# A shift of a matrix by half its rows and columns: both column halves of a row in one DMA

## The chip, the core and the metric

The kernel runs on one core of one Trainium2 chip. It uses no compute engine for its work: the matrix is moved from device memory to device memory by the core's 16 DMA engines, which are told what to copy by instructions ("issues") on a queue of SyncE, called SP in the profile. The metric is the device time of one execution in microseconds. Each kernel is run several times and the median is given. One further execution is taken with the hardware profiler; its trace has a record of every instruction, of every packet that a DMA engine moved, and of every report that a DMA has landed.

## The reference

```python
"x": np.random.randn(8192, 8192).astype(np.float32)

def reference(x: np.ndarray) -> np.ndarray:
    return np.fft.ifftshift(x)
```

With even sizes, the shift moves every element by half the rows and half the columns, round the edge: `out[r, c] = x[(r + 4096) % 8192, (c + 4096) % 8192]`. The four quadrants of the matrix change places across the diagonals. Nothing is calculated. The input has 8192 x 8192 x 4 bytes = 268.4 MB, all of which is read once and written once. A row is 32 KB long; half a row, 16 KB, is contiguous both in the source and in the destination.

## The kernel before

`R` and `C` are the rows and columns, 8192 each; `hr` and `hc` are their halves, 4096 (lines 21 to 23). The loop on line 35 takes `rows = ENGINES * apart` = 64 output rows at a time, 128 times. For each block of 64 rows the loop on line 36 issues four DMAs, one per quarter of the row. A quarter is `piece = hc // 2` = 2048 columns, 8 KB. The quarters are taken in the order of their first output column: 0, `hc`, `piece`, `hc + piece`; that is, the first quarter, the third, the second, the fourth.

Numbering the quarters 0 to 3, the first DMA of a block writes quarter 0 and reads quarter 2 of the rows 4096 further on; the second writes quarter 2 and reads quarter 0; the third writes 1 and reads 3; the fourth writes 3 and reads 1.

The helper `copy` (lines 25 to 29) builds one DMA. Its access pattern has two dimensions, `[[C, rows], [1, piece]]`: 64 rows, 32 KB from one to the next, and 2048 contiguous elements in each. So a DMA holds 64 pieces of 8 KB, 512 KB in all. The 64 rows are divided over the 16 engines, four rows each (`apart = 4`). An engine copies a piece as one packet; after its share of a DMA it writes a small packet that raises the DMA's semaphore by one.

There are 128 x 4 = 512 DMAs, all issued on SyncE's queue, `nc.sync`, in program order; line 26 is the line that the profile gives for an issue. There is no explicit wait in the kernel's text. The tile framework gives the DMAs eight semaphores in turn, and an issue that takes a semaphore again first waits until the DMA that used it eight issues earlier has landed. That is the wait put down to line 26. At the end of the program, line 63, SyncE waits for the last DMAs.

Nothing in the program depends on the order in which DMAs land, as no two of them touch the same bytes.

Of the kernel before, what the change touches and what calls it, by code (L numbers as in the profile page):

```python
# [1 line left out]

# [4 lines left out]


ENGINES = 16  # L10


@with_exitstack
def kernel(
    ctx: ExitStack,
    tc: tile.TileContext,
    x: bass.AP,
    out: bass.AP,
):
    nc = tc.nc  # L20
    R, C = x.shape
    hr = R // 2
    hc = C // 2

    def copy(queue, row, col, dims):
        queue.dma_start(
            out=bass.AP(out.tensor, out.offset + row * C + col, dims),
            in_=bass.AP(x.tensor, x.offset + (row + hr) % R * C + (col + hc) % C, dims),
        )


    apart = 4
    piece = hc // 2
    rows = ENGINES * apart
    for row in range(0, R, rows):
        for col in (0, hc, piece, hc + piece):
            copy(nc.sync, row, col, [[C, rows], [1, piece]])


# [1 line left out]
_INS = ['x']  # L41
_OUTS = [((8192, 8192), 'float32')]


def kernel(**inputs):
    import numpy as _np
    import concourse.bacc as _bacc
    import concourse.tile as _tile
    from concourse import mybir as _mybir
    from concourse.bass_utils import run_bass_kernel_spmd as _run  # L50

    nc = _bacc.Bacc("TRN2", target_bir_lowering=False, num_devices=1)  # L52
    arrays, args = {}, []
    for name in _INS:
        a = _np.ascontiguousarray(inputs[name])
        if a.dtype.kind in "iu":
            a = a.astype(_np.int64)
        arrays[f"in_{name}_dram"] = a
        args.append(nc.dram_tensor(f"in_{name}_dram", a.shape, _mybir.dt.from_np(a.dtype), kind="ExternalInput").ap())
    for i, (shape, dtype) in enumerate(_OUTS):  # L60
        dt = _mybir.dt.from_np(_np.dtype(dtype))
        args.append(nc.dram_tensor(f"out_{i}_dram", shape, dt, kind="ExternalOutput").ap())
    with _tile.TileContext(nc) as tc:
        kernel(tc, *args)
    r = _run(nc, [arrays], core_ids=[0])
    got = tuple(r.results[0][f"out_{i}_dram"] for i in range(len(_OUTS)))
    return got[0]
```

## Time and profile before

| What | Value |
|---|---|
| Median of 3 runs | 813.25 us (812.37 to 813.68) |
| The profiled execution: its own time | 811.93 us |
| The profiled execution: span of the core | 810.2 us |
| Share of the span in which the 16 DMA engines had a packet of the kernel's queue | 99.1% |
| Packets of the kernel's queue | 40,960 |
| Bytes moved per second, one way | 331 GB/s |
| Issues | 512, of 512 KB |
| From issue to landing, median (lowest, highest) | 12.6 us (4.0, 13.2) |
| Time that SyncE's queue waited at line 26 for earlier DMAs | 525.9 us |

How to read it: the span runs from the first instruction of the core to the last; the execution's own time is a little longer, since it has what lies around them. The DMA line of the page cuts the span into 40 equal slices and gives the mean busy share of the 16 DMA engines in each, as a digit in tenths; the line under it gives the bytes that they moved. A packet counts as busy from its start to its end, also while it makes no progress. "GB/s" of the engines counts a copied byte once; the line on the memory counts it twice, as a byte read and a byte written. The waits are those of SyncE's queue; "us in total, times, longest us" follow the colon. The issue line gives the count, the size of one and the median time to its landing. The four GpSimd instructions on the page set constants at the start, and the kernel does not use them.

### The profile page before, as it was taken

Reading aid. Unit: us, or ns where it says so; the run is one execution under the profiler, and the core shown is the slowest. Engines: PE = TensorE matmul, PEld = TensorE weight load, DVE = VectorE, ACT = ScalarE, POOL = GpSimd, SP = SyncE. Lnnn points to the kernel's source line nnn. Section 1 sums busy time; section 2 is a strip of 40 time slices with the busy share of each in tenths; the row PEclk is TensorE's granted clock in tenths of the full one; section 3 lists DMA queues with packets and bytes.
Section 4 is the critical chain, followed back from the end, with each engine's and each line's share of the span. In section 5 each row is a group of like instructions: output and inputs, shape, how many; then the busy total and the mean of one; then the engine's idle time right before and its main releaser. Section 6 shows DMA issues by size and latency. Waiting matters only on the chain. (4 is left out here: it accounts for less than half of the span.)

```text
span 810.2 us, 557 instructions
## 1 busy us (share of the span) xinstructions
POOL 0.2 (0%) x4
## 2 busy tenths in 40 slices
POOL 0000000000000000000000000000000000000000
DMA  8999999999999999999999999999999999999998
GB/s 301 334 328 339 330 335 336 334 329 335 337 336 331 331 335 335 329 335 331 339 333 329 339 336 331 339 330 331 337 336 326 337 330 335 333 328 335 326 328 299
DMA packets 40964, 268.50 MB, mean 331 GB/s; under 512 B 8192, under 2 KB 8192, under 8 KB 8192
## 3 DMA queue, kind: packets, MB, share of 16 engines
q1 hardware_dynamic: 40960, 268.47, 99.1%
q14 instruction: 4, 0.03, 0.0%
HBM read 268.44 MB, written 268.44 MB: 663 GB/s over the span
## 5 line engine op out<-in xcount | busy, mean ns | idle before, releaser
L52 POOL MEMSET const-bfloat16-1.0<- 128x1 bf16 x1 | 0.1, 102 | 0.0
L52 POOL MEMSET const-uint8-127<- 128x1 uint8 x1 | 0.1, 102 | 0.0
L52 POOL MEMSET const-float32-0.0<- 128x1 f32 x1 | 0.1, 99 | 0.2 <-issue 0.2
L52 POOL MEMSET const-float32-1.0<- 128x1 f32 x1 | 0.1, 99 | 0.0
## 6 DMA issues: line engine op xcount, KB each, us to landing
out_dram<-in_x_dram SPq DMA_DIRECT2D x512, 512.0 KB, 12.6
```

Source lines behind the costliest of these rows:

```text
L52: nc = _bacc.Bacc("TRN2", target_bir_lowering=False, num_devices=1)
```

## The change

One DMA now takes the same quarter of both halves of 64 rows. The helper `both` replaces `copy`. Its access pattern has three dimensions: 64 rows; two pieces `hc` columns (16 KB) apart; 2048 contiguous elements. In the destination the second piece lies `hc` columns after the first, in the source `hc` columns before it, since the halves change places. The loop over the columns has two steps, 0 and `piece`, where it had four. So there are 128 x 2 = 256 DMAs of 128 pieces, 1 MB each, on the same queue. The 64 rows are still divided over 16 engines, four rows each, and an engine has eight pieces in a DMA: for each of its rows the piece in the left half of the output and then the piece in the right half.

```diff
-    def copy(queue, row, col, dims):
+    def both(queue, row, col, rows, piece):
+
         queue.dma_start(
-            out=bass.AP(out.tensor, out.offset + row * C + col, dims),
-            in_=bass.AP(x.tensor, x.offset + (row + hr) % R * C + (col + hc) % C, dims),
+            out=bass.AP(out.tensor, out.offset + row * C + col, [[C, rows], [hc, 2], [1, piece]]),
+            in_=bass.AP(
+                x.tensor,
+                x.offset + (row + hr) % R * C + hc + col,
+                [[C, rows], [-hc, 2], [1, piece]],
+            ),
         )
...
     for row in range(0, R, rows):
-        for col in (0, hc, piece, hc + piece):
-            copy(nc.sync, row, col, [[C, rows], [1, piece]])
+        for col in (0, piece):
+            both(nc.sync, row, col, rows, piece)
```

## The prediction

> **What bounds the kernel now.** I read the page from the top: span, share by slice, DMA queue, DMA issues; then SyncE's waits, the windows at the two ends of the span, and last the single packet records.
>
> ```profile
> span 810.2 us, 557 instructions
> ...
> DMA  8999999999999999999999999999999999999998
> ...
> DMA packets 40964, 268.50 MB, mean 331 GB/s; under 512 B 8192, under 2 KB 8192, under 8 KB 8192
> ...
> q1 hardware_dynamic: 40960, 268.47, 99.1%
> ...
> HBM read 268.44 MB, written 268.44 MB: 663 GB/s over the span
> ...
> out_dram<-in_x_dram SPq DMA_DIRECT2D x512, 512.0 KB, 12.6
> ```
>
> No compute engine takes part. The 16 DMA engines have a packet in hand 99.1% of the span, in every slice. 40,960 packets over 512 DMAs are 80 each: 64 pieces of 8 KB and 16 small ones that report completion, one from each engine. A DMA lands 12.6 us after its issue, but 810.2 / 512 = 1.58 us pass per DMA, so 12.6 / 1.58 = 8 are in flight.
>
> ```profile
> SPq L26 <- DMA out_dram<-in_x_dram: 525.9, 502, 2.0
> SPq L63 <- DMA out_dram<-in_x_dram: 11.5, 4, 7.1
> ```
>
> SyncE's queue waits 525.9 us at line 26 for an older DMA to land before it issues the next: it runs ahead and is held back, it does not hold the engines up. The instruction itself takes 511 ns (median for line 26), 512 x 0.511 = 262 us.
>
> ```profile
> 0.73:2.14 1.41, 0.00 (x0) 1.00 0.00 0
> 2.14:3.00 0.86, 0.00 (x0) 1.00 1.19 171
> ...
> 806.00:807.00 1.00, 0.00 (x0) 1.00 0.95 344
> 807.00:808.00 1.00, 0.00 (x0) 1.00 0.74 254
> 808.00:809.00 1.00, 0.00 (x0) 1.00 0.18 74
> 809.00:810.20 1.20, 0.00 (x0) 1.00 0.00 0
> ```
>
> The windows (stretch, length, GpSimd, clock, DMA share, GB/s) show what is not copying: 1.41 us from the first issue to the first packet, a drain of about 2 us as engines run dry one by one, 1.2 us at the end.
>
> "Busy" is not "fast". In the packet records the commonest 8 KB packet takes 309 ns, and 60% take that; 40% take longer, 511 ns on average; the mean is 389.9. Packets of one engine follow each other 3 ns before the end of the last, so with none slow the copy would take 32,768 / 16 x 0.306 = 627 us. The other some 180 us is time in which an engine holds a packet that is held up: (389.9 - 309) x 2,048 = 166 us of it directly. What holds it is outside the engines; that it is the memory is my reading. So the bound is the rate at which memory serves 16 engines that read and write together, 663 GB/s, and the change can matter mainly through the 81 ns of mean excess. The Trainium skill (HBM Reference, Specifications) gives about 716 GB/s for the memory that a core pair shares; 663 is 93% of it, by which an estimate of the least time is 537 MB / 716 = 750 us.
>
> **The change part by part.** Sums are against the profiled execution, 811.93 us (span 810.2 and 1.73 around it), 1.32 us under the median of the three runs, 813.25.
>
> *Issues.* 512 DMAs of 64 pieces become 256 of 128. If the 511 ns go with the pieces, 8 ns each, an issue takes 1.02 us; the engines need 2 x 1.58 = 3.15 us for a DMA, so SyncE still waits some 2.1 us each time. Cost nothing; cover is the copying, and it is gone only if an issue took over 3.15 us. Nothing else is queued on SyncE but the next issue, and the final wait of line 63, which grows from 11.5 us to about 23 with eight DMAs of twice the size in flight, behind copying that must be done anyway.
>
> *Start.* The first packet comes 1.41 us after the first issue began, whose instruction took 0.63. If packets wait until the whole DMA is described, 64 more pieces add up to 0.6; if not, nothing. I take 0.3.
>
> *Completion packets.* 8,192 become 4,096, so 256 fewer on each engine. Each lasts 9 ns, and the next packet starts 6 after its start: 256 x 6 = 1.5 us. Where the memory is the limit, engine time set free turns into waiting, so between 0 and 1.5 (2.3 at 9 ns); by the 60% of packets that go at full pace, I take -0.9. There may be a little more behind them: the 8 KB packets that can be told to follow a completion packet directly take 395 ns, 5 over the mean, 256 x 5.5 = 1.4 us at most. The Trainium skill (DMA: Bandwidth & Descriptors, Rules for kernel authors) speaks for 1 MB or more per DMA, since each has a fixed cost. Were its two microseconds paid 512 times in a row, they would exceed the whole time: here seven other DMAs cover them, and the rows leave only those few microseconds.
>
> *Order of the pieces.* This is what the time hangs on. An engine takes four rows of each DMA. Before, it copies four pieces 32 KB apart in address, then the other half of the same rows, then the next quarter. After, it copies a row's piece and then that row's piece 16 KB further, while the source goes 16 KB back. The bytes, sizes and rows touched by 16 engines in a few microseconds stay nearly alike: the 16 landings of a DMA are 1.76 us apart in the median, longer than a DMA lasts, so engines already mix two DMAs. The alternation within one engine is shown nowhere in the trace, so I bound it by the four kinds of step from one DMA to the next. Sort the 32,768 data packets by start and take the 33rd of each 64 as the middle of a DMA; from middle to middle is (mean of about 123, standard error about 11 ns):
>
> - same rows, other half (columns 0 to hc): 1,564 ns
> - next quarter (hc to piece): 1,573
> - same rows, other half (piece to hc + piece): 1,602
> - next 64 rows: 1,559
>
> Mean 1,574.6. The two steps to the other half of the same rows average 1,583.1, the two others 1,566.1. The difference, 17 ns, is about one and a half standard errors of it: a hint and no proof. The nearest row to the new order is the first pair, where some engines are in one half of the rows and some in the other: if all copying went so, 512 x (1,583.1 - 1,574.6) = +4.4 us. Ends: all like the slowest step, 512 x (1,602 - 1,574.6) = +14; all like the fastest (1,550 for next 64 rows, with the cut three quarters into a DMA), 512 x (1,550 - 1,574.6) = -12.6. I take +4.4, for being the nearest.
>
> *Tail.* Every engine has the same bytes as before. The drain is set by how far engines drift apart, and 1.76 us is far less than the 12.6 us of queue, so the queue does not limit the drift and a longer one does not widen it: 0, at worst another 1.8.
>
> Sum: 0.3 - 0.9 + 4.4 = +3.8; 811.93 + 3.8 = 815.7, and with the 1.32 to the median **817.0 us**.
>
> **The rivals.**
>
> *The order of the pieces is indifferent.* For it: the four steps lie within 2.8% of each other, though columns and rows change differently in each. Then 813.25 + 0.3 - 0.9 = 812.7, within 0.2%, which is 1.6 us and about what a measurement of this kernel can tell from no change. Against it: two percent of 807 us is 16 us, and memory that is held up in 40% of the packets is unlikely not to notice a new order at all.
>
> *The alternation eases the memory (faster).* Two pieces of one row within some 0.8 us instead of 1.6 could be served better than pieces of different rows. Place: the 40% slow packets. Price: if all copying goes like the fastest step, -12.6, with the other terms 813.25 - 12.6 - 0.6 = 800; half of that, 806. It decides from the point where the mean packet falls under about 389 ns, since 1.6 us / 2,048 packets is 0.8 ns. Against it: the steps that stay in the same rows are, if anything, the slower ones, and the step to new rows is the fastest.
>
> *Engines get in each other's way.* With a DMA of eight packets an engine, drift of 4.5 packets (1.76 us / 0.39) keeps all engines within one DMA and one pair of quarters for longer. If the slow packets go from 40% to 44%, the excess grows by a tenth: 8 ns x 2,048 = 17 us, 829; to 50%, 20 x 2,048 = 41 us, 854. For it: the slowest step, 1,602, is one within a pair of quarters. Against it: the other such step takes 1,564.
>
> *The change doesn't do what it says.* Were the pieces split over the two halves and not the rows, two engines would carry a DMA and the time would be several times as long; were an engine given all of one half first, the order would be the old one and the time 812.7.
>
> **How the numbers follow.** Somewhat slower, by up to 14 us and around 817: 0.38. Engines in each other's way, 829 and more: 0.10. Indifferent or the old order, 812.7: 0.18. Faster, 800 to 811: 0.33. A split over few engines: 0.01. So slower 0.49, same 0.18, faster 0.33. The range goes from 801 (the fastest step throughout, 800, nearly) to 830 (the slowest step, +14, start and tail, +2.4, and the lesser price of engines in each other's way); about 0.06 lies below and 0.10 above. The likeliest case alone runs from 815 to 828, the slowest step throughout without tail.
>
> **What would show it.** Packets 32,768 + 4,096 + the four that fetch instructions; 256 issues of 1 MB, landing after about 25 us; an issue of about 1.0 us; SyncE's wait still most of its time. If I am right the mean 8 KB packet takes 392 ns (4.4 us / 2,048 = 2.1 ns more), GB/s drops evenly over the slices to about 330, the DMA share stays at 99%, and the two ends keep their lengths. A first packet after 1.41 + 0.6 us would show the start at its upper end; a drain of 4 us the tail. A mean packet under 389 ns makes the forecast wrong on the fast side; idle engines (a share under 98%) would mean that issues or the queue matter, which I have ruled out.

## The result and the profile after

The changed kernel takes 811.08 us (median of 14 runs, 809.99 to 812.37), the kernel before 813.16 us (14 runs beside them, 811.43 to 816.31). The ratio is 0.9972 with a 95% interval of 0.9964 to 0.9981: the change makes the kernel 0.28% faster, 2.1 us, and the interval stays clear of no change. I had forecast 817.0, that is 0.45% slower.

The page of the changed kernel, the same lines as shown of before:

```profile
span 808.7 us, 301 instructions
...
DMA  8999999999999999999999999999999999999998
...
DMA packets 36866, 268.47 MB, mean 332 GB/s; under 512 B 4096, under 2 KB 4096, under 8 KB 4096
...
q1 hardware_dynamic: 36864, 268.45, 99.3%
...
HBM read 268.44 MB, written 268.44 MB: 664 GB/s over the span
...
out_dram<-in_x_dram SPq DMA_DIRECT2D x256, 1024.0 KB, 25.1
```

The change does what it says: 32,768 data packets as before, 4,096 completion packets in place of 8,192, 256 DMAs of 1 MB that land after 25.1 us, so still eight in flight. The engines have a packet in hand in all slices, and the rate went from 663 to 664 GB/s of reading and writing together. Nothing large moved anywhere.

SyncE's waits after, and the group of its issues before and after (lowest, median and highest duration in ns, first and last start in us):

```profile
SPq L27 <- DMA out_dram<-in_x_dram: 634.0, 248, 3.2
SPq L68 <- DMA out_dram<-in_x_dram: 24.1, 4, 15.2
```

```profile
L26 SPq DMA_DIRECT2D out_dram<-in_x_dram x512: 511/511/695, 0.7 to 797.2; - x171
```

```profile
L27 SPq DMA_DIRECT2D out_dram<-in_x_dram x256: 562/562/682, 0.7 to 783.1; - x128
```

The queue is held back by landings for 634 us, more than before, and the last wait doubled as foreseen. An issue of twice the pieces takes 562 ns, and before it took 511. The number of pieces is not what adds the 51 ns: the old order in 256 DMAs (below) has 128 pieces in a DMA too, in the old pattern of two dimensions, and its issues take 511.

The windows at the two ends (stretch, length, GpSimd, clock, DMA share, GB/s):

```profile
0.73:2.14 1.41, 0.00 (x0) 1.00 0.00 0
2.14:3.00 0.86, 0.00 (x0) 1.00 0.95 162
...
805.00:806.00 1.00, 0.00 (x0) 1.00 0.88 336
806.00:807.00 1.00, 0.00 (x0) 1.00 0.30 123
807.00:808.00 1.00, 0.00 (x0) 1.00 0.02 8
```

The start is as long as before; the drain is some 1.5 us earlier, and about as long. So the gain was made on the way and not at the ends. The single packet records say where, as far as one execution of each can:

| Per engine, profiled execution | Before | After |
|---|---|---|
| First packet's start to last packet's end | 806.90 us | 805.36 us |
| Sum of packet times | 803.06 us | 803.07 us |
| of it completion packets (9 ns each) | 4.6 us | 2.3 us |
| Mean 8 KB packet | 389.9 ns | 391.0 ns |
| 8 KB packets over 312 ns | 40.0% | 40.9% |
| Time with no packet in hand | 11.5 us | 9.2 us |

The last row is an estimate: the first row, less the second, plus 3 ns for each packet of an engine (2,560 and 2,304), by which a packet usually starts before the end of the one before it. By the windows, more than 1 us of it is the drain at the end, before and after. In this execution the 2.3 us of completion packets that are gone came back as longer data packets, 1.13 ns x 2,048 = 2.3 us, and what made it shorter is 2.3 us less of idle moments, less 0.8 us of overlap that went with the fewer packets.

This split is not firm. The three later profiles of the changed kernel have 8.0 us without a packet (chip 2, mean packet 392.0 ns), 8.9 and 7.6 us (chip 9, 396.3 and 397.2 ns). Another kernel of the experiments, the new order in 512 DMAs with two neighbouring rows an engine, has 11.3 us in one profile (chip 9) and 9.0 in another (chip 6). So the row moves by up to some 2 us from one profile of a kernel to another, as much as the gain, and of the kernel before there is only one.

### The profile page after: what moved, and what is told of

Read it like the earlier page. It is cut to its first block, busy times and chain, and to the rows that moved or that the text cites. A ratio compares the mean times of both kernels' runs of the same rounds, so it can differ in the third digit from the quotient of the medians.

```text
span 808.7 us, 301 instructions
## 1 busy us (share of the span) xinstructions
POOL 0.2 (0%) x4
## 2 busy tenths in 40 slices
DMA packets 36866, 268.47 MB, mean 332 GB/s; under 512 B 4096, under 2 KB 4096, under 8 KB 4096
## 6 DMA issues: line engine op xcount, KB each, us to landing
out_dram<-in_x_dram SPq DMA_DIRECT2D x256, 1024.0 KB, 25.1
```

## The experiments

Four kinds of cause stood open: that the two pieces of a row in succession make the gain (order), that the halved number of DMAs does (count), that the longer queue does, or that it belongs to the chip. In a fixed copy of 268 MB with about eight DMAs in flight, half as many DMAs are always twice as large and the queue twice as long, so the runs below can't tell count from queue; what they say of the count holds for both together. The runs came to lie on four chips, numbered in the results; each kernel is compared with runs of the kernel before on the same chip, and with the other kernels run beside it. The kernel before takes 812.7 us on chip 2, as in the first comparison, but 822.6 to 823.9 on chips 6, 7 and 9.

**The changed kernel again, and 1024 DMAs in both orders (chip 9).** The old order is cut by rows, so that every engine keeps its four rows and their order:

```diff
-    def copy(queue, row, col, dims):
+    def copy(queue, row, col, n, piece):
+        dims = [[apart * C, ENGINES], [C, n], [1, piece]]
...
         for col in (0, hc, piece, hc + piece):
-            copy(nc.sync, row, col, [[C, rows], [1, piece]])
+            for first in (0, 2):
+                copy(nc.sync, row + first, col, 2, piece)
```

The new order is cut to one row an engine:

```diff
-            out=bass.AP(out.tensor, out.offset + row * C + col, [[C, rows], [hc, 2], [1, piece]]),
+            out=bass.AP(
+                out.tensor,
+                out.offset + row * C + col,
+                [[apart * C, ENGINES], [hc, 2], [1, piece]],
+            ),
...
-                [[C, rows], [-hc, 2], [1, piece]],
+                [[apart * C, ENGINES], [-hc, 2], [1, piece]],
...
-            both(nc.sync, row, col, rows, piece)
+            for first in range(apart):
+                both(nc.sync, row + first, col, piece)
```

> The changed kernel again, beside the others on the same chip. Count theory (the gain of 2.1 us is that of 256 fewer DMAs, some 8 ns on each engine for a completion packet and what follows it) and order theory (the gain is that of two pieces of one row in succession) both expect 811, 2 us under the kernel before. Were the gain a matter of the chip or the day, it would be gone here.

Measured: 821.82 us against 822.56, ratio 0.9994 (0.9984 to 1.0004). The gain is not to be seen here.

> The old order of pieces on every engine, each DMA cut in two (two of an engine's four rows), so 1024 DMAs of 256 KB. Count theory: 512 more DMAs at 8 ns, +4.1 us, 817.3. Order theory: the order is that of the kernel before, so 813.2, or little more. Queue theory (the gain is that of 8 MB queued in place of 4): 2 MB are queued here, so slower than 813.2 by an amount that need not follow the count.

Measured: 824.70 us, ratio 1.0029 (1.0015 to 1.0043): 2.1 us slower, half of what the count theory's 8 ns per DMA ask for.

> The new order of pieces on every engine, each DMA cut in four (one of an engine's four rows, its two pieces), so 1024 DMAs of 256 KB. Count theory: the same time as the old order with 1024 DMAs, 817.3, whatever the order. Order theory: 2 us faster than that one. My forecast's term for the order (+4.4 us for the new one): 4.4 us slower than that one.

Measured: 822.53 us, ratio 1.0005 (0.9995 to 1.0014). Rows, count, queue and number of packets are those of the old order in 1024 DMAs, and the new order is 2.2 us faster (by the means of 8 and 11 runs, 1.3 to 3.1). The page has it as well, with the same packets in both. First the old order, then the new:

```profile
q1 hardware_dynamic: 49152, 268.50, 99.6%
...
HBM read 268.44 MB, written 268.44 MB: 652 GB/s over the span
```

```profile
q1 hardware_dynamic: 49152, 268.50, 99.6%
...
HBM read 268.44 MB, written 268.44 MB: 653 GB/s over the span
```

This speaks for the order and against my term for it, which has the other sign. And it speaks against the count: with 768 DMAs more than the changed kernel, the new order loses 0.7 us in the medians. Beside the kernel before, though, the cut into 1024 DMAs costs the old order 2 us and brings the new one nothing: the contrast of the orders is shown at 1024 DMAs, and not at the 512 and 256 of the two kernels.

**The new order in 512 DMAs, two neighbouring rows an engine.** The changed kernel with `apart = 2`.

> The changed kernel with two rows an engine in place of four: two pieces of one row in succession, 512 DMAs of 512 KB of 32 rows each. Count theory: the time of the kernel before, 813.2. Order theory: that of the changed kernel, 811. It also brings the engines' rows together (64 KB apart and not 128 KB), so a time outside 810 to 814 would be put down to that.

Measured: 822.83 us, ratio 1.0002 (0.9993 to 1.0011) on chip 9: the kernel before, neither better nor worse. By itself that is the count theory's number, but on a chip where the changed kernel has nearly no gain either. It is 0.7 us over the changed kernel (means, 0.0 to 1.3), as much as the new order in 1024 DMAs (0.6): here the step from 256 to 512 DMAs has the whole difference.

**Once more (chip 9), and the old order in 256 DMAs.** The last is the kernel before with `apart = 8`.

> The changed kernel a third time, since the gain of 0.28% of the first comparison was 0.06% (-0.04 to 0.16) in the second, on a chip where both kernels take 1.1% longer. If the gain belongs to the change, it lies between, 0.1 to 0.3%; if it belongs to the chip, it is 0.28% where the kernel before takes 813 us and near zero where it takes 822.

Measured: 821.88 us against 822.83, ratio 0.9989 (0.9980 to 0.9999): a gain, of some two fifths of the first one's size.

> The old order in 1024 DMAs again. It was 0.29% slower than the kernel before (0.15 to 0.43). Count theory and queue theory: the same again. If the difference is one of the chip, it can have another sign.

Measured: 824.33 us, ratio 1.0023 (1.0008 to 1.0037), the same again.

> The new order in 1024 DMAs again, against the old order in 1024 DMAs beside it: it was 2.2 us faster than that one, and 0.7 us slower than the changed kernel with 256. Order theory: again some 2 us under the old order. Count theory: as slow as the old order.

Measured: 822.81 us, ratio 1.0004 (0.9996 to 1.0013). It is 1.8 us under the old order (means, 1.0 to 2.6) and 0.8 us over the changed kernel (0.3 to 1.3). Both differences have come twice.

> The kernel before with eight rows an engine in place of four: 256 DMAs of 1 MB and eight packets an engine as in the changed kernel, but all eight pieces in one quarter of the columns. Count theory: the time of the changed kernel, 0.1 to 0.3% under the kernel before. Order theory: the time of the kernel before. The engines' rows lie 256 KB apart and not 128, which a time over 0.3% from both would be put down to.

Measured: 823.84 us, ratio 1.0018 (0.9998 to 1.0038), with runs from 820.1 to 831.8. With the changed kernel's count, DMA size and queue, the old order has none of the gain; it is some 2 us behind the changed kernel. Its engines lie 256 KB apart, so this is not the order alone.

**Still fewer DMAs, and three probes of the bound (chip 7, the last repeated on chip 2).** Ahead of the probes, the changed kernel with `apart = 8`, 128 DMAs of 2 MB.

> The changed kernel with eight rows an engine: 128 DMAs of 2 MB, 16 packets an engine, two pieces of a row in succession. If fewer DMAs and a longer queue are worth anything, another step of the kind from 512 to 256, about half as large: 0.05 to 0.15% under the changed kernel. If the order of pieces is the gain, the time of the changed kernel, about 0.1% under the kernel before where that takes 822 us.

Measured: 822.17 us, ratio 0.9988 (0.9975 to 1.0002): not to be told from the changed kernel on chip 9. Its issues are another matter:

```profile
L27 SPq DMA_DIRECT2D out_dram<-in_x_dram x128: 600/5958/14508, 0.7 to 777.0; - x128
...
DMA to landing us min/median/max: 9.3/42.6/49.8
```

There is no wait on line 27 left among SyncE's waits; instead the issue itself takes 5.96 us. At 820 / 128 = 6.4 us per DMA, 42.6 us are 6.6 DMAs in flight and not eight, so something other than the eight semaphores holds the issue back; no run shows what. It costs nothing that the time shows: the kernel is not slower for it.

The first probe moves the engines apart, each on 256 rows of its own:

```diff
-    def copy(queue, row, col, dims):
+    def copy(queue, row, col, piece):
+        dims = [[hr // ENGINES * C, ENGINES], [C, apart], [1, piece]]
...
-    for row in range(0, R, rows):
-        for col in (0, hc, piece, hc + piece):
-            copy(nc.sync, row, col, [[C, rows], [1, piece]])
+    for half in (0, hr):
+        for row in range(half, half + hr // ENGINES, apart):
+            for col in (0, hc, piece, hc + piece):
+                copy(nc.sync, row, col, piece)
```

> The kernel before with the 16 engines 8 MB apart (256 rows) and not 128 KB (4 rows): 512 DMAs of 512 KB, four rows and the same order of quarters on every engine. If the memory is indifferent to where 16 streams lie, 822 or 813, as the kernel before. If it is the memory that holds the slow packets, and its rate depends on addresses, clearly off, by over 2%; the Trainium skill (DMA: Bandwidth & Descriptors, Latency and other measured facts) has such copies at half their rate for rows 4 MB apart.

Measured: 1,826 us (four runs, 1,729 to 1,923), 2.2 times the kernel before, with the same packets and the same steps on every engine:

```profile
DMA packets 40964, 268.50 MB, mean 155 GB/s; under 512 B 8192, under 2 KB 8192, under 8 KB 8192
...
q1 hardware_dynamic: 40960, 268.47, 98.0%
...
HBM read 268.44 MB, written 268.44 MB: 311 GB/s over the span
```

The page is that of the fastest of the four. The engines are about as busy as before (98.0%), at half the rate; the mean 8 KB packet takes 825 ns. The only thing that differs is where the 16 streams lie. The Trainium skill's row on this (DMA: Bandwidth & Descriptors, Latency and other measured facts) has half the rate at a row pitch of 4 and 8 MiB; here rows of one engine are 32 KB apart and only the engines are 8 MB apart, and the rate is 155 / 331 = 0.47. So the trace agrees on the size, and in this kernel the distance between the engines is enough for it.

The second probe takes half a row as one piece, `piece = hc` and columns 0 and `hc`, four packets of 16 KB an engine and 256 DMAs.

> The kernel before with half a row as one piece: 256 DMAs of 1 MB, four packets of 16 KB an engine. If a packet's start costs anything beside its bytes, faster than the changed kernel, at most by 16,384 / 16 x 3 ns = 3 us. If the memory sets the rate, within 0.3% of the kernel before.

Measured: 827.06 us, ratio 1.0058 (1.0036 to 1.0080). Half as many packets and half as many DMAs as before, and slower by 0.58%: what is saved per packet and per DMA does not decide here. Which part of the loss belongs to the larger packet and which to the order of addresses, both of which this edit changes, the run does not tell.

The last probe reads without writing back:

```diff
-    def copy(queue, row, col, dims):
...
+    pool = ctx.enter_context(tc.tile_pool(name="rows", bufs=8))
...
-            copy(nc.sync, row, col, [[C, rows], [1, piece]])
+            t = pool.tile([rows, piece], mybir.dt.float32)
+            nc.sync.dma_start(
+                out=t[:, :],
+                in_=bass.AP(
...
+            if row + rows == R:
+                nc.sync.dma_start(
...
+                    in_=t[:, :],
+                )
```

> All 512 pieces are read into on-chip memory and only the last block of 64 rows is written out, so the output is left out almost wholly: it shows the packets without writes to memory. If slow packets come from memory that is read and written at once, nearly all 8 KB packets take 309 ns and the time is about 2,048 x 0.306 = 627 us and some 5. If the engines themselves are slow at times, 40% of the packets stay slow and the time stays near 813.

Measured: 1,298 us, which neither view allowed for. The packets took 629 ns nearly all, and the rate was 209 GB/s. A DMA of 64 rows fills 64 of the 128 on-chip partitions. The probe was repeated with `apart = 8`, 128 rows a DMA, which also makes a DMA twice as large:

> The loading kernel again with 128 rows a DMA, so that the on-chip side is written over all 128 partitions and not 64, which alone doubled every packet to 629 ns. Writing out is again left out but for the last block. If slow packets come from memory that is read and written at once, nearly all packets take 309 ns and the time is about 2,048 x 0.306 = 627 us and some 5; if they come from the engines or from reading alone, some 40% of the packets stay slow.

Measured (chip 2, one run): 653 us, some 20 over the 632 expected, as an engine has 2,080 packets with those written out, at 314 ns each. The loads:

```profile
DMA packets 37442, 272.66 MB, mean 419 GB/s; under 512 B 4160, under 2 KB 4160, under 8 KB 4160
...
q1 hardware_dynamic: 37440, 272.65, 100.7%
...
HBM read 268.44 MB, written 4.19 MB: 419 GB/s over the span
```

The mean packet takes 314 ns and the 99th percentile 321; the slow packets, a mean of 511 ns and 40% of all in the kernel before, are gone. So the engines are not slow by themselves and neither is reading alone: the slow packets come with the writing to device memory. Whether it takes reading and writing together, or writing alone would do, was not tried.

**The parts of the gain where the gain is (chip 2), and a last look (chip 6).** The new order in 512 DMAs, with the same four rows for every engine:

```diff
-            out=bass.AP(out.tensor, out.offset + row * C + col, [[C, rows], [hc, 2], [1, piece]]),
+            out=bass.AP(out.tensor, out.offset + row * C + col, [[2 * C, rows], [hc, 2], [1, piece]]),
...
-                [[C, rows], [-hc, 2], [1, piece]],
+                [[2 * C, rows], [-hc, 2], [1, piece]],
...
-            both(nc.sync, row, col, rows, piece)
+            for first in (0, 1):
+                both(nc.sync, row + first, col, rows // 2, piece)
```

> The new order with the count of the kernel before: 512 DMAs of 512 KB, four packets an engine, engines 128 KB apart as before; an engine copies both pieces of its first and third row, then in the next DMA those of its second and fourth. Order theory (two pieces of a row in succession are the gain): the gain of the changed kernel, whole. Count theory (fewer completion packets are the gain): the time of the kernel before. My term for the order: +4.4 us.

Measured: 814.33 us against 812.70, ratio 1.0020 (1.0009 to 1.0032): slower than both kernels. Of the three views only my term for the order had this direction, at over twice the size. The kernel has the pairs of the new order and the count of the old, but an engine goes from its first row to its third. Two pieces of one row in succession are therefore not enough; which rows the engines are in, and which come next, matters as much.

> The changed kernel beside the run of the new order in 512 DMAs. Where the kernel before takes 822 us: 0.06 to 0.12% under it, as twice already. Where it takes 813: 0.2 to 0.36% under it, if the gain goes with the chip. Count theory: some 0.1% or 0.9 us under the new order in 512 DMAs, by 256 x 6 ns x 60%.

Measured: 810.75 us, ratio 0.9973 (0.9961 to 0.9985). The first result stands, on a chip of its kind.

> The new order in 1024 DMAs of one row an engine, third time, so that the new order stands on one chip with 256, 512 and 1024 DMAs. Count theory: in steps of 0.9 us per 256 DMAs, so 2.7 us over the changed kernel. It was 0.7 and 0.9 us over it; that again if the count matters little.

Measured: 812.23 us, ratio 0.9996 (0.9987 to 1.0006), and 1.3 us over the changed kernel (means, 0.7 to 1.9). 768 DMAs more cost 1.3 us, so 0.4 us per 256 if each costs the same; the two comparisons on chip 9 give 0.2 and 0.3. Of the changed kernel's gain on this chip, 1.9 us by the means, 0.6 is left (-0.2 to 1.3), which is not clear of zero.

> The old order in 1024 DMAs, the same rows on every engine as the new order in 1024 DMAs. Where the kernel before takes 813 us, the new order in 1024 was 0.04% under it (-0.13 to 0.06). Order theory: the old order stands 0.2 to 0.3% above the kernel before, as on the chip of 822 us, so some 2 us above the new order at equal count. If order were nothing, 0.04% under the kernel before, as the new one.

Measured on chip 6: 823.87 us against 823.85, ratio 1.0008 (0.9996 to 1.0020): not above the kernel before beyond its interval, unlike on chip 9.

> The new order in 512 DMAs with two neighbouring rows an engine. Between the changed kernel (256 DMAs) and the new order in 1024 the times differ by 0.23% where the kernel before takes 813 us; if the count acts evenly, this one stands a third of the way, at 0.19% under the kernel before there, and the order has by far the larger part of the gain. If the count has all of the gain, it takes the time of the kernel before.

Measured beside it: 822.75 us, ratio 0.9984 (0.9970 to 0.9999): a gain at the count of the kernel before, near the 0.19% expected, but on a chip of 823 us and with neighbouring rows 64 KB apart. On chip 9 the same kernel had none.

All of it in one table: change of the time against the kernel before on the same chip. The 95% intervals reach 0.1 to 0.2 points to either side.

| Order | Rows of an engine in a DMA | DMAs | Kernel before at 813 us | Chip 9 (822 us) | Chips 6 and 7 (823 us) |
|---|---|---|---|---|---|
| new | 4 (the changed kernel) | 256 | -0.28%, -0.27% | -0.06%, -0.11% | |
| new | 8 | 128 | | | -0.12% |
| new | 2, neighbours | 512 | | +0.02% | -0.16% |
| new | 2, every other row | 512 | +0.20% | | |
| new | 1 | 1024 | -0.04% | +0.05%, +0.04% | |
| old | 8 | 256 | | +0.18% | |
| old | 2 | 1024 | | +0.29%, +0.23% | +0.08% |
| old, pieces of 16 KB | 4 | 256 | | | +0.58% |

## Why the forecast was wrong

*The bound* was read rightly. The engines hold packets all the time, the issue queue has slack, and the packets are slow only where device memory is written as well as read (314 ns on the mean without the writing, 390 with it), at a rate that depends on addresses (2.2 times the time with the engines 8 MB apart). That it takes both at once is not shown, as writing alone was not tried.

*Issues, start, tail.* SyncE's wait stayed most of the span, at no cost; the issue takes 562 ns and not 1.02 us. The first packet came 1.44 us after the first issue, 0.03 later and not 0.3. The tail is unchanged, as taken. All three are small.

*Completion packets*, -0.9 us. By the slope of the new order from 256 to 1024 DMAs the halving is worth 0.2 to 0.4 us; by the run with 512 on chip 9 it is worth 0.7 (0.0 to 1.3). In the new order the direction was right. The idea that engine time set free turns into waiting fits the profiled execution, in which all 2.3 us came back in the data packets, and not only the 40% that I took off; but the mean packet differs by nearly as much between two profiles of the changed kernel on one chip (396.3 and 397.2 ns), so it is not shown.

*The order of the pieces*, +4.4 us, is the step that failed, by sign and size. I took the steps from one DMA to the next within the same rows (1,564 and 1,602 ns) as the nearest row and the first pair's average as its price, a difference of 17 ns, one and a half standard errors, and I said that it was a hint. It did not come again: the same reckoning on the three later traces in the old order (1024 DMAs, two of them to a step) gives -14 and -8 ns on chip 9 and +4 on chip 6, with a standard error of 11 or 12 each. In the changed kernel the total moved by -2.1 us; taking off what the slope gives to the count, the order is left with some -1.7, an estimate by subtraction that no run isolates. The clean contrast, 1024 DMAs in the two orders, gives -2.2 and -1.8 us on chip 9. Nowhere did pairs in neighbouring rows lose 4 us. But a single figure for the order cannot stand either: at 512 DMAs the new order with neighbouring rows was at +0.02% (chip 9) and -0.16% (chip 6), and with skipped rows at +0.20% (chip 2). A step between DMAs, where some engines are in one half of the rows and others in the other, does not price an order that every engine follows all the time.

*The rivals.* The measured time lies within my range, on the side that I gave a third of the chances. The rival that came true in direction is that the alternation eases the memory, at a sixth of its price of -12.6 us; that the alternation is the reason is not shown, since with every other row skipped it lost time. "Indifferent", 812.7, was nearest in time, and is wrong by 1.6 us. The point from which the faster case was to decide, a mean packet under 389 ns, failed outright: the mean rose to 391.0, and to 392.0 in a second profile, while the kernel got faster. I had forgotten that the packets are not all of an engine's time: some 11.5 us per engine had no packet in hand, as much as everything in dispute.

*What stays open.* Why the order acts as it does is not settled: no run shows which addresses get in each other's way in memory. That the gain is 0.27 to 0.28% where the kernel before takes 813 us and 0.06 to 0.11% on chip 9, which takes 822, has been seen twice each; the reason was not found. On chip 9 the new order at 512 DMAs was no better than the old one, so there the little gain of the changed kernel may be the count's, or the longer queue's, which always changed with it. The contrast of the orders in 1024 DMAs was not made on a chip of 813 us, and on chip 6 only the old order of the two was run. So of the 2.1 us it stays open how much is the order's and how much the count's and the queue's. No version beat the changed kernel beyond the intervals.

## What to carry to other kernels

In a copy from device memory to device memory with all engines busy, look at the rate and not at the busy share: with the engines 8 MB apart they are 98% busy at half the rate. The packets are no better judge of a small change: the changed kernel is the faster one with the longer mean packet and the larger share of slow ones. In this kernel the place of the engines' streams made a factor of two, and the number of DMAs hardly anything (128 to 1024 DMAs of the new order lie within 0.3% of the kernel before), so a merge of DMAs should be judged by the order of addresses that it makes, too. A difference between steps that is not clear of its own error is no price (here three later traces gave -14, -8 and +4 ns for the +17 of the first): take zero for it and keep the sign open, and compare small gains on more than one chip.

## What was not expected of the hardware

- An issue costs 511 ns in the pattern of two dimensions, with 64 pieces (the kernel before) as with 128 (old order in 256 DMAs), and 562 to 571 in the patterns of three dimensions, with 128 pieces (the changed kernel), 64 or 32 (new order in 512 and 1024 DMAs): it goes with the pattern and not with the pieces, until issues block as in the next point.
- With 17 packets an engine in a DMA (128 DMAs), issues block for 5.96 us at 6.6 DMAs in flight, before the wait for the eighth landing is reached.
- The same kernel takes 812.7 us on one chip and 822.6 to 823.9 on three others, a spread of 1.4%, five times the effect under study.
- Loads in DMAs of 64 rows, into 64 on-chip partitions, ran at 209 GB/s, and in DMAs of 128 rows, into 128, at 419.
